# One decoder step on one core: padded queries copied by VectorE, and a causal mask moved out of the matrix products of the state-space mixer

## The chip, the core and the metric

The program runs on one core of one Trainium2 chip. The metric is the device time of one execution in microseconds, the median of three runs, and lower is better. The engines of the core run beside each other, each through its own queue in order: TensorE (PE, with its weight loads PEld), VectorE (DVE), ScalarE (ACT), GpSimd (POOL) and SyncE (SP, which here only issues transfers). An instruction that waits holds up all that stands behind it in its queue.

## What is computed

The reference is one step of a two-layer decoder over 512 prompt tokens and 8 sample tokens, 520 columns in all. Layer 0 mixes tokens by sparse attention with 16 heads, layer 1 by a Mamba-2 scan with 32 heads; each mixer is followed by a squared-ReLU MLP. Of the attention, the change touches the prompt's two masked score products (selected keys and window keys), and of the scan this:

```python
seg = a_cum[:, :, :, None] - a_cum[:, :, None, :]
decay = jnp.exp(jnp.where(causal, seg, NEG))
cb = jnp.einsum('bclgn,bcsgn->bclsg', cc, bc)
y_diag = jnp.einsum('bclsg,bclsgr,bcsgrp->bclgrp', cb, decay, xdt)
...
final, prev = lax.scan(step, init_state.astype(f32), ...)
y_off = jnp.einsum('bclgn,bcgrpn,bclgr->bclgrp', cc, prev, jnp.exp(a_cum))
```

For a sample the scan is one step: state = state * exp(dt a) + (x dt) B, and y = sum over n of state * C.

## The kernel before, in words

All products with weights split each weight tile into a high and a low fp32r part (`split`, lines 407 and after: ACT writes `hi`, DVE writes `lo`, tiles `wh`) and multiply three times (`unit`, L323). One product of 1024 by 128 weights is 48 matmuls that write a tile `a`; two such tiles and six `wh` tiles exist. The instructions of each engine are put in order by a scheduler when the program is built, so that the order of the queues is not the order of the code; a change in one stage reorders others.

**Attention** (`attention`, L1021, one item for each of 8 head pairs `i`, 4 query tiles `t` of 128 and 2 halves `e`, 64 items). `att_qk` (L937) makes the scores of an item: for both key sets one product with the high keys (`sc<-kv,q`), one with the low keys (`sc<-kv,c`), and the mask as a product of the identity with `negqR` (`sc<-c,c`). The low keys of two heads lie in one tile, so the second product takes queries that are zero in the other head's 64 rows: a padded tile `qz[e]`, 128 by 128, into which POOL copies the 64 rows of this item (L945, `c<-q`). There is one such tile for each `e`, so a copy waits for the products of the item two before. POOL also issues the stores of cached keys and values (`out_kwin`, L357) and the loads of the selected pages (`wh<-in_selv`, L395). `att_soft`, `att_scale`, `att_tr` and `att_pv` follow some items later; the sample group's attention and the modulation products are woven in.

**Mixer** (`ssd`, in the order of `SSD_SEQ`: four groups `bc`, each with four pairs of heads). `ssd_bc` (L1465) computes B, C and `cb`, the product of B and C by chunks of 128 tokens. `ssd_pair` (L1507) does one pair `q` of heads, 16 in all:

- Two PSUM tiles `ps[e]`, each the cumulated decay spread over 128 rows by a product with one column of `e2R`, plus the mask as a product of the identity with `negsR`: four matmuls of 512 columns (`s<-c,c`).
- For each head four ACT operations `M<-s,c` (exponential with the negated decay `nac` as bias, 128 columns each), then one DVE product `M<-M,g` with `cb`.
- POOL builds `sp`, and one matmul of 384 columns (`s<-c,sp`) gives the decay of both heads for their own 64 rows, of which ACT takes the exponential `E`.
- Then the transposes of X (`s<-c,x`), the chunk states (`s<-xd,g`), the diagonal part (`s<-M,xd`), the off-diagonal part (`s<-g,st`).
- For each of the 8 samples: ACT scales B (`xb<-bc,x`), DVE updates the state (`ss<-ss,c,xb`, L1463) and multiplies it by C with an accumulated sum (`xb,ys<-ss,bc`), 128 elements each. The sums `ys` enter the sample columns of `y`.

`ssd_gate` multiplies `y` by the gate `z` (`y<-y,z`), squares it and splits it into `yh` for the output products; after the last pair the norm of the mixer (`s<-c,yss`, `s<-c,z`) needs all of `y`. The PSUM pool `s` has four tiles.

Of the kernel before, what the change touches and what calls it, by code (L numbers as in the profile page):

```python
# [11 lines left out]
F32R = mybir.dt.float32r  # L12
# [15 lines left out]
_o = 0  # L30
# [6 lines left out]
def shape_constants():  # L37
    c = np.zeros((128, NCONST), np.float32)

    def put(name, a):  # L40
        o, w = CONST_AT[name]
        c[:a.shape[0], o:o + w] = a

    i = np.arange(128)
    put('ident', np.eye(128, dtype=np.float32))
    put('negq', np.where(i[None, :] <= i[:, None], 0.0, NEG))
    put('tri', (i[:, None] <= i[None, :]).astype(np.float32))
    put('negs', np.where(i[:, None] <= i[None, :], 0.0, NEG))
    t = np.arange(4)[None, :, None] * 128 + i[:, None, None]
    ok = (16 * np.arange(32)[None, None, :] + 31 <= t) & (np.arange(32) < 31)  # L50
    put('cadd', np.where(ok, 0.0, NEG).reshape(128, 128))
    put('cmul', ok.astype(np.float32).reshape(128, 128))
    j, hc = i // 32, i % 32
    gp, r, e = hc // 8, (hc // 2) % 4, hc % 2
    live = hc < 16
    g = 2 * gp + e
    b = np.arange(8)
    put('selb', np.stack([(b[:, None] == 4 * k + j[None, :]) & live[None, :] for k in range(2)], 1)
        .astype(np.float32).reshape(8, 256))
    put('gsel', ((np.arange(16)[None, :] == (g * 4 + r)[:, None]) & live[:, None]).astype(np.float32))  # L60
# [201 lines left out]
class Step:  # L262
# [391 lines left out]
    def setup_late(self):  # L654
        I = self.I
        wg = self.tile('s', [128, 384])
        self.aux(wg, I['w_gate'])
        self.wg = [self.tile('kv', [128, 384], F32R) for _ in range(2)]
        self.copy(self.wg[0], wg)
        self.tt(self.wg[1], wg, self.wg[0], ALU.subtract)  # L660
        t = self.tile('s', [128, 256])
        self.aux(t[:, 0:128], I['const'][:, CONST_AT['negq'][0]:CONST_AT['negq'][0] + 128])
        self.aux(t[:, 128:256], I['const'][:, CONST_AT['negs'][0]:CONST_AT['negs'][0] + 128])
        self.negqR = self.const([128, 128], F32R, self.pn)
        self.vcopy(self.negqR, t[:, 0:128])
        self.negsR = self.const([128, 128], F32R)
        self.vcopy(self.negsR, t[:, 128:256])
        u = self.U('np')
        self.load_consts(u[:, 0:256], 'selb', 'selb', self.aux)
        self.gt = u[:, 256:448].rearrange("p (a b) -> p a b", a=4)  # L670
        self.load_consts(self.U('np'), 'cadd', 'jc', self.aux)
# [265 lines left out]
    def att_qk(self, n):  # L937
        i, t, e = n
        gp = i // 4
        w = (t + 1) * 128  # L940
        q = self.Q[i][e][:, t * 128:(t + 1) * 128]
        r = slice(64 * e, 64 * e + 64)

        qz = self.qz[e]
        self.nc.gpsimd.tensor_copy(qz[r], q[r])  # L945
        one = self.tile('sc', [128, 2, 256]) if w <= 256 else None
        self.S[n] = []
        for k in range(2):
# [73 lines left out]
    def attention(self, fill, rate):  # L1022

        items = [(i, t, e) for i in range(8) for t in range(4) for e in range(2)]
        N = len(items)
        self.S, self.P, self.PT = {}, {}, {}
        self.qz = [self.const([128, 128], F32R, self.pn) for _ in range(2)]
        for z in self.qz:
            self.nc.gpsimd.memset(z.bitcast(F32), 0.0)
        cg = [self.att_cmp(i) for i in range(0, 8, 2)]  # L1030
        for n in range(N + PV + 1):
            if n < N:
                i, t, e = items[n]
                next(cg[n // 16], None)
                self.att_qk(items[n])
            if 0 <= n - TR < N:
                self.att_tr(items[n - TR], 0)
            m = n - PV
            if 0 <= m < N and m % 2 == 1:
                self.att_pv(items[m][0], items[m][1])  # L1040
            if 0 <= n - TR < N:
                self.att_tr(items[n - TR], 1)
            if n < N:
                self.att_soft(items[n])
            if 0 <= n - 1 < N:
                self.att_scale(items[n - 1])
            fill.step(rate)
# [310 lines left out]
    def dt_fin(self, ps):  # L1358
# [47 lines left out]
        self.copy(ac, p[:, 0:128])  # L1406

        m = self.m[0].rearrange("p a b -> p (a b)")
        self.nac, self.cd, self.dtde = (m[:, ck(n)].rearrange("p (c h) -> p c h", c=4) for n in range(3))
        fl = "p c h -> p (c h)"  # L1410
        self.ts(self.nac.rearrange(fl), p[:, 0:128], -1.0)
        self.copy(ae, p[:, 128:256])
        self.act(self.cd.rearrange(fl), p[:, 128:256], AF.Exp)
        self.tt(ae, ae, ac, ALU.subtract)
# [50 lines left out]
    def ssd_bc(self, g, first):  # L1465
# [7 lines left out]
        for c in range(4):  # L1473
            self.mm(p[:, ck(c)], B[:, ck(c)], C[:, ck(c)], True, True)
        cb = self.tile('g', [128, 512])
        self.copy(cb, p)
        p = self.tile('s', [128, 512])
        for c in range(4):
            self.tr(p[:, ck(c)], B[:, ck(c)])
# [24 lines left out]
    def ssd_pair(self, g, t, X, G, w):  # L1504
# [4 lines left out]
        M = []  # L1509
        ps = [self.tile('s', [128, 512]) for _ in range(2)]  # L1510
        for e in range(2):
            self.mm(ps[e], self.e2R[:, 2 * q + e:2 * q + e + 1].to_broadcast([128, 128]), self.ac2, True, False)
        for e in range(2):
            self.mm(ps[e].rearrange("p (c l) -> p c l", c=4), self.identR,
                    self.negsR[:, None, :].to_broadcast([128, 4, 128]), False, True)
        for e in range(2):
            h = 2 * q + e
            p = ps[e]
            m = self.tile('M', [128, 512])
            for c in range(4):  # L1520
                self.act(m[:, ck(c)], p[:, ck(c)], AF.Exp, bias=self.nac[:, c, h:h + 1])
            self.tt(m, m, cb, ALU.mult)
            M.append(m)
        sp = self.tile('sp', [128, 2, 64], F32R)
        self.nc.gpsimd.tensor_copy(sp, self.e2R[:, 2 * q:2 * q + 2, None].to_broadcast([128, 2, 64]))
        p = self.tile('s', [128, 512])
        self.mm(p[:, 128:512], sp.rearrange("p a b -> p (a b)"), self.ac2[:, 128:512], True, True)
        E = self.tile('E', [128, 512])
        self.act(E[:, 128:512], p[:, 128:512], AF.Exp)

        p = self.tile('s', [128, 512])
        for c in range(4):
# [44 lines left out]
        for b in range(8):  # L1577
# [1 line left out]
            x = self.tile('xb', [128, 128])  # L1579
            self.act(x, bc[0][:, b], AF.Copy, scale=x8[:, b:b + 1])  # L1580
            self.pool_stt(v, v, self.sdb[:, q, 1, b:b + 1], x, ALU.mult, ALU.add)
            self.stt(x, v, 1.0, bc[1][:, b], ALU.mult, ALU.mult, accum_out=ys[:, b:b + 1])
        self.store(self.O['ssm_s'][q], w.rearrange("p b n -> p (b n)"))
        self.stt(y[:, 512:T], xs[:, 2 + t], self.dsk[:, q:q + 1], ys, ALU.mult, ALU.add)
        return y
# [295 lines left out]
    def build(self, stop=None):  # L1881
        self.make_plan()
        base = {'n': 1, 'r': 1}
        with self.phase('n', {'kv': 16, 'np': 9, 's': 5, 'pcm': 1, 'ptc': 1, 'ptsc': 1, 'ad': 1, 'sq': 1, 'ssq': 1, 'x7': 's'}) \
                as self.pn, self.phase('np', {'t': 2, 'o': 1, 'f': 1}, PSUM):
            ap = contextlib.ExitStack()
            ap.enter_context(self.products_phase('ap1'))
# [11 lines left out]
        with self.tc.tile_pool(name='e', bufs=1) as self.pe:  # L1899
# [4 lines left out]
                    return  # L1904
                h = self.boundary(('n', 'r'), BOUND_CGS[1], 'f')
            with self.phase('s', {'g': 5, 'cv': 2, 'x': 2, 'th': 2, 'xd': 3, 'st': 2, 'M': 2, 'E': 1, 'y': 1, 'z': 1,
                                  'acc': 8, 'bc': 1, 'ss': 2, 'xb': 3, 'yss': 1, 'yh': 8, 'sp': 1,
                                  'sq': 'M', 'x7': 'M', 'ssq': 'st', 'ad': 'xd', 'dt': 'acc'}) as self.ps, \
                    self.phase('sp', {'s': 4}, PSUM), self.products_phase('ap4'), \
                    self.tc.tile_pool(name='dr', bufs=2, space=bass.MemoryType.DRAM) as self.pd:  # L1910
# [59 lines left out]
```

## Time and profile before

| | us |
|---|---|
| median of 3 runs | 1711.87 (1711.11 to 1712.05) |
| the profiled execution, its own time | 1709.68 |
| its span, first to last instruction | 1708.0 |
| PE busy in the span | 1661.1 (97%) |
| DVE busy | 978.6 (57%) |
| ACT busy | 762.3 (45%) |
| POOL busy | 117.9 (7%) |

The span of the profile is the time between the first and the last instruction; the execution's own time has 1.7 us around it. The attention lies from about 207 to 420 us, the first MLP to 870, the pairs of the mixer from 917 to 1282, the second MLP from 1320 on. Busy times of PE are modelled from pipelined matmuls: two matmuls overlap in the record, and what one costs the queue is read from the distance of two starts.

### The profile page before, as it was taken

The page shows a single profiled execution, that of the slowest core. Times are in us where ns is not written, and L with a number is a line of the kernel's source. Part 1 is how long each engine was busy: PE and PEld are TensorE (multiplying, and loading weights), DVE is VectorE, ACT ScalarE, POOL GpSimd, SP SyncE. Part 2 cuts the span into 40 slices and gives each one's busy share as a digit, 9 for nine tenths or more (in the row PEclk, how much of TensorE's full clock was granted, in tenths as well). Part 3 has the DMA queues.
Part 4 walks back from the last instruction along what each step waited for, and adds up shares of the span by engine and source line. Part 5 has one row for each costly group of instructions (what it writes and reads, how often), then busy time and mean ns, then how long its engine had stood idle before and what let it go on. Part 6 is the DMA issues. An engine that isn't in the chain of part 4 may idle for free.

```text
span 1708.0 us, 34635 instructions
## 1 busy us (share of the span) xinstructions
PE 1661.1 (97%) x13846; PEld 1544.8 (90%) x13846; DVE 978.6 (57%) x2442; ACT 762.3 (45%) x1624; POOL 117.9 (7%) x284
## 2 busy tenths in 40 slices
PE   7999999999999999999999999999999999999997
PEld 6799876667989999999989999999997999999997
DVE  2543377776464343433469977979797543434344
ACT  3534376666443132322446766647564432323231
POOL 2000112310000000000001101101010000000000
PEclk9999999999999999999999999999999999999999
DMA  9723656545433524244433352343425223323221
GB/s 323 270 87 100 216 201 227 167 143 196 139 116 107 175 97 136 87 136 136 136 131 119 105 181 83 128 143 129 144 79 183 70 92 88 98 87 99 87 87 51
DMA packets 72114, 229.87 MB, mean 135 GB/s; under 512 B 8770, under 2 KB 15218, under 8 KB 71186
## 3 DMA queue, kind: packets, MB, share of 16 engines
q1 hardware_dynamic: 62546, 198.45, 35.2%
q0 software_dynamic: 8832, 28.16, 4.5%
q8 instruction: 109, 1.79, 0.4%
q10 hardware_dynamic: 576, 1.05, 0.2%
q14 instruction: 51, 0.42, 0.1%
HBM read 204.02 MB, written 23.61 MB: 133 GB/s over the span
## 4 chain that ended last, share of the span: by engine, by line
PE 76%; DVE 2%; issue 1%; ACT 1%; SPq 1%; POOLq 0%; DMA 0%; POOL 0%; DVEq 0%; ACTq 0%
PE a L323 64%; PE s L323 5%; PE f L323 2%; PE o L323 1%; PE sc L323 1%; PE t L327 1%; PE s L327 1%; DVE c L345 0%; SPq L395 0%; SPq L393 0%; POOLq L393 0%; PE f L327 0%; DVE g L345 0%; DMA w<-in_selk_dram 0%; DVE wh L336 0%
## 5 line engine op out<-in xcount | busy, mean ns | idle before, releaser
L323 PE MATMUL a<-h,wh 128*128 128x256 f32 x5952 | 746.6, 285 | 5.9 <-ACT t L333 1.6
L323 PEld LDWEIGHTS a<-h,wh 128*128 128x128 f32 x5952 | 726.9, 190 | 13.1 <-issue 3.8
L330 ACT ACTIVATE wh<-w 128x1024 fp32r<-128x1024 f32 x212 | 224.6, 1060 | 513.7 <-PE a L323 479.3
L336 DVE TENSOR_TENSOR wh<-w,wh 128x1024 fp32r<-128x1024 f32 x212 | 259.6, 1224 | 269.8 <-ACT wh L330 266.8
L323 PEld LDWEIGHTS a<-hid,wh 128*128 128x128 f32 x3072 | 370.2, 188 | 5.0 <-issue 4.2
L323 PE MATMUL a<-hid,wh 128*128 128x256 f32 (+1 forms) x3072 | 373.6, 283 | 0.0
L336 DVE TENSOR_TENSOR t<-a,c 128x8 f32<-128x8 f32 x72 | 12.0, 166 | 215.8 <-PE a L323 215.8
L323 PE MATMUL a<-yh,wh 128*128 128x256 f32 (+1 forms) x768 | 98.4, 285 | 0.3 <-DVE acc L336 0.3
L323 PEld LDWEIGHTS a<-yh,wh 128*128 128x128 f32 x768 | 93.7, 188 | 1.9 <-ACT wh L330 0.8
L330 ACT ACTIVATE hid<-t 128x520 fp32r<-128x520 f32 x64 | 40.8, 639 | 84.5 <-DVE t L336 84.5
L330 ACT ACTIVATE h<-t 128x128 f32<-128x128 f32 (+3 forms) x128 | 52.8, 441 | 51.7 <-PE t L327 51.1
L333 ACT ACTIVATE h<-sc,m 128x128 f32<-128x128 f32 (+3 forms) x128 | 66.6, 529 | 10.4 <-DVE m L340 7.4
L336 DVE TENSOR_TENSOR hid<-t,hid 128x520 fp32r<-128x520 f32 x64 | 44.7, 699 | 42.3 <-ACT hid L330 42.3
L333 ACT ACTIVATE xb<-bc,x 128x128 f32<-128x128 f32 x128 | 45.4, 413 | 29.2 <-DVE xb L345 21.3
L345 DVE SCALAR_TENSOR_TENSOR c<-a,c,c 128x512 f32<-128x512 f32 (+1 forms) x74 | 53.8, 728 | 1.8 <-PE a L323 1.8
L327 PE MATMUL t<-c,h 128*128 128x128 f32 x320 | 53.7, 281 | 0.9 <-DVE h L340 0.4
L327 PEld LDWEIGHTS t<-c,h 128*128 128x128 f32 x320 | 35.1, 141 | 13.8 <-issue 8.6
L323 PE MATMUL sc<-kv,q 128*128 128x128 f32 (+3 forms) x128 | 47.0, 379 | 0.0
L323 PEld LDWEIGHTS a<-q,wh 128*128 128x128 f32 x384 | 46.2, 188 | 0.8 <-issue 0.8
L323 PE MATMUL a<-q,wh 128*128 128x256 f32 (+1 forms) x384 | 46.5, 283 | 0.0
L323 PE MATMUL sc<-kv,c 128*128 128x128 f32 (+3 forms) x128 | 41.3, 334 | 4.3 <-POOL c L945 4.3
L340 DVE TENSOR_SCALAR h<-h,z 128x128 f32<-128x128 f32 (+3 forms) x128 | 44.4, 384 | 1.3
(367 smaller groups left out, 1903.1 us busy)
## 6 DMA issues: line engine op xcount, KB each, us to landing
w<-in_w_dram SPq DMA_DIRECT2D x128, 512.0 KB, 3.5
w<-in_ada_w_dram SPq DMA_DIRECT2D x80, 512.0 KB, 3.6
w<-in_w_ssd_dram SPq DMA_DIRECT2D x40, 512.0 KB, 3.6
w<-in_w_nsa_dram SPq DMA_DIRECT2D x20, 512.0 KB, 3.7
ss<-in_ssm_dram SPq DMA_DIRECT2D x16, 512.0 KB, 4.5
out_ssm_s_dram<-ss POOLq DMA_DIRECT2D x16, 512.0 KB, 3.1
w<-in_w_sout_dram SPq DMA_DIRECT2D x16, 512.0 KB, 4.1
cm<-in_cmp_dram SPq DMA_DIRECT2D x24, 256.0 KB, 4.2
```

Of the source, the lines that this page charges most:

```text
L323: self.nc.tensor.matmul(out, lhsT, rhs, start=start, stop=stop, skip_group_check=True)
L327: self.nc.tensor.transpose(out, in_, self.C('ident')[0:k, 0:k])
L330: self.nc.scalar.activation(out, in_, AF.Copy, **kw)
L333: self.nc.scalar.activation(out, in_, f, **kw)
L336: self.nc.vector.tensor_tensor(out, a, b, op=op)
L340: self.nc.vector.tensor_scalar(out, a, s1, None, op0=op0)
L345: self.nc.vector.scalar_tensor_tensor(out, a, s, b, op0=op0, op1=op1, **kw)
```

## The change

- Attention: the padded tiles are 128 by 256, hold two query tiles, and DVE copies into them ahead, once for two items (`att_pad`): 32 copies of 64 by 256 in place of POOL's 64 of 64 by 128.
- Mixer, mask: `cb` is multiplied by the 0/1 triangle when it leaves PSUM (a DVE product instead of an ACT copy, 4 in all). The mask product with `negsR` goes. So that the exponential can't overflow above the diagonal, ACT first takes Relu of the negated difference, 4 operations a head, and then the exponential of the negated result in one operation of 512 columns.
- Mixer, `E`: ACT takes it from the two `ps[e]` (64 rows each) and not from a product of its own; `sp`, its copy and its matmul go.
- Mixer, samples: the eight products with C become one DVE operation of 1024 elements into a tile `vc` and one DVE sum. `xb` has 2 buffers instead of 3.
- Room: `negsR` goes, `ptsc` shares the buffer of `ad`.

```diff
     def att_qk(self, n):
...
-        qz = self.qz[e]
-        self.nc.gpsimd.tensor_copy(qz[r], q[r])
+        qz = self.qz[e][:, (t % 2) * 128:(t % 2) * 128 + 128]
...
+    def att_pad(self, i, t, e):
+        r = slice(64 * e, 64 * e + 64)
+        self.vcopy(self.qz[e][r], self.Q[i][e][r, t * 128:t * 128 + 256])
...
     def attention(self, fill, rate):
...
+        for e in range(2):
+            self.att_pad(0, 0, e)
...
                 self.att_qk(items[n])
+                if t % 2 and n + 2 < N:
+                    self.att_pad(*items[n + 2])
...
     def ssd_bc(self, g, first):
...
-        self.copy(cb, p)
+        self.tt(cb.rearrange("p (c l) -> p c l", c=4), p.rearrange("p (c l) -> p c l", c=4),
+                self.C('tri')[:, None, :].to_broadcast([128, 4, 128]), ALU.mult)
...
     def ssd_pair(self, g, t, X, G, w):
...
-            self.mm(ps[e], self.e2R[:, 2 * q + e:2 * q + e + 1].to_broadcast([128, 128]), self.ac2, True, False)
-        for e in range(2):
-            self.mm(ps[e].rearrange("p (c l) -> p c l", c=4), self.identR,
-                    self.negsR[:, None, :].to_broadcast([128, 4, 128]), False, True)
+            self.mm(ps[e], self.e2R[:, 2 * q + e:2 * q + e + 1].to_broadcast([128, 128]), self.ac2, True, True)
...
-                self.act(m[:, ck(c)], p[:, ck(c)], AF.Exp, bias=self.nac[:, c, h:h + 1])
+                self.act(m[:, ck(c)], p[:, ck(c)], AF.Relu, scale=-1.0, bias=self.ac[:, c, h:h + 1])
+
+            self.act(m, m, AF.Exp, scale=-1.0)
             self.tt(m, m, cb, ALU.mult)
...
-        sp = self.tile('sp', [128, 2, 64], F32R)
-        self.nc.gpsimd.tensor_copy(sp, self.e2R[:, 2 * q:2 * q + 2, None].to_broadcast([128, 2, 64]))
-        p = self.tile('s', [128, 512])
-        self.mm(p[:, 128:512], sp.rearrange("p a b -> p (a b)"), self.ac2[:, 128:512], True, True)
         E = self.tile('E', [128, 512])
-        self.act(E[:, 128:512], p[:, 128:512], AF.Exp)
+        for e in range(2):
+            r = slice(64 * e, 64 * e + 64)
+            self.act(E[r, 128:512], ps[e][r, 128:512], AF.Exp)
...
-            self.stt(x, v, 1.0, bc[1][:, b], ALU.mult, ALU.mult, accum_out=ys[:, b:b + 1])
+        vc = self.tile('vc', [128, 8, 128])
+        self.tt(vc, w, bc[1], ALU.mult)
+        self.nc.vector.tensor_reduce(ys, vc, AX.X, ALU.add)
```

The scheduler moves instructions in both stages. Three places matter below.

POOL's queue before, at the start of the attention (`c<-q` the padded copy, `out_kwin` a store of cached keys or values):

```order
L357 DMA out_kwin_dram<-wh_3396 128x1024
L945 COPY c_2383<-q_996 64x128
L357 DMA out_kwin_dram<-wh_3402 128x1024
L945 COPY c_2384<-q_997 64x128
L945 COPY c_2383<-q_996 64x128
```

The copies stand behind stores that wait for a load. DVE's queue now, at the same place (`im` and `pcm` belong to other parts of the attention, `m<-sc` is the row maximum of the scores):

```order
L335 TENSOR_TENSOR pcm_2391<-pcm_2391,mcm_2455 128x512
L335 TENSOR_TENSOR im_2476<-im_2476,c_2444 128x12
L347 COPY c_2380<-q_993 64x256
L335 TENSOR_TENSOR c_2444<-c_2444,c_1507 128x64
L965 TENSOR_REDUCE m_2496<-sc_2482 128x2
```

The copy leaves the queue in which it stood behind stores that wait for loads, and stands in DVE's behind small operations; it now serves the third query tile, since the first two are padded before the attention begins.

ACT's queue in the mixer, at the fifth pair, before (`M` a head's decay matrix, `x` a convolution):

```order
L333 ACTIVATE M_12741<-s_12735,c_99 128x128
L333 ACTIVATE x_12718<-cv_12713,c_7351,c_7349 128x512
L333 ACTIVATE M_12741<-s_12735,c_99 128x128 x3
L333 ACTIVATE M_12747<-s_12736,c_99 128x128 x4
L333 ACTIVATE E_12757<-s_12755 128x384
L330 ACTIVATE xd_12766<-s_12759,c_11223 128x64 x8
```

`E` and `xd` follow the eight `M` at once. ACT's queue now, at the same pair:

```order
L332 ACTIVATE M_12672<-s_12668,c_99 128x128
L332 ACTIVATE x_12651<-cv_12646,c_7316,c_7314 128x512
L332 ACTIVATE M_12672<-s_12668,c_99 128x128 x3
L332 ACTIVATE M_12679<-s_12669,c_99 128x128
L332 ACTIVATE M_12672<-M_12672 128x512
L332 ACTIVATE M_12679<-s_12669,c_99 128x128 x3
L332 ACTIVATE E_12686<-s_12668 64x384
L332 ACTIVATE M_12679<-M_12679 128x512
L332 ACTIVATE E_12686<-s_12669 64x384
L332 ACTIVATE th_12656<-x_12651 128x512
L332 ACTIVATE cvt_12663<-xs_12277 128x8
L329 ACTIVATE xd_12696<-s_12689,c_11188 128x64 x8
```

Three more operations stand between a pair's first `M` and the `xd` that its diagonal product also needs, and PE's queue holds more products with weights between the `s<-c,c` and the first `s<-M,xd` of a pair: 42 where 19 stood at this pair, 57 where 29 stood at the last.

DVE's queue at the last pair of the mixer before (`y<-y,z` is the last product with the gate):

```order
L1463 SCALAR_TENSOR_TENSOR ss_16460<-ss_16460,c_11288,xb_16564 128x128
L345 SCALAR_TENSOR_TENSOR z_16625<-z_16625,a_16576 128x520
L345 SCALAR_TENSOR_TENSOR xb_16564,ys_16535<-ss_16460,bc_15334 128x128
L345 SCALAR_TENSOR_TENSOR y_16529<-xs_15164,c_7358,ys_16535 128x8
L336 TENSOR_TENSOR y_16529<-y_16529,z_16625 128x520
```

One product with C and the gate's first step lie between the last state update and `y`. DVE's queue now, at the same pair:

```order
L1466 SCALAR_TENSOR_TENSOR ss_16305<-ss_16305,c_11253,xb_16399 128x128
L335 TENSOR_TENSOR vc_16402<-ss_16305,bc_15203 128x1024
L335 TENSOR_TENSOR wh_16485<-w_16476,wh_16484 128x1024
L1585 TENSOR_REDUCE ys_16377<-vc_16402 128x8
L344 SCALAR_TENSOR_TENSOR y_16371<-xs_15033,c_7323,ys_16377 128x8
L335 TENSOR_TENSOR y_16371<-y_16371,z_16462 128x520
```

Three operations of 1024 elements, one of them a weight split, stand between the last state update and the last `y<-y,z`, where two small ones of this pair and the gate's stood. In PE's queue 22 products with weights stand between the last `s<-M,xd` and the norm's `s<-c,z`, where 55 stood before.

## Rows read from the trace of the kernel before

**Rows 1.** The page: busy time by engine, and the chain that ended last.

```profile
PE 1661.1 (97%) x13846; PEld 1544.8 (90%) x13846; DVE 978.6 (57%) x2442; ACT 762.3 (45%) x1624; POOL 117.9 (7%) x284
...
PE 76%; DVE 2%; issue 1%; ACT 1%; SPq 1%; POOLq 0%; DMA 0%; POOL 0%; DVEq 0%; ACTq 0%
```

**Rows 2.** Stretches: length, busy PE, PEld, DVE, ACT, POOL (instructions), clock, DMA, GB/s.

```profile
207.00:420.00 213.00, 203.68 (x1872) 143.22 (x1870) 158.00 (x578) 139.17 (x442) 46.94 (x123) 0.99 0.55 192
212.80:216.20 3.40, 3.36 (x15) 3.36 (x15) 0.99 (x5) 0.57 (x3) 1.34 (x4) 0.51 0.78 316
917.00:1000.00 83.00, 81.44 (x673) 77.50 (x671) 77.85 (x236) 59.34 (x163) 10.02 (x24) 1.00 0.42 144
1020.00:1103.00 83.00, 82.80 (x678) 79.17 (x677) 67.05 (x183) 53.17 (x139) 9.05 (x21) 1.00 0.37 122
917.00:1282.00 365.00, 363.06 (x2990) 345.95 (x2989) 313.20 (x918) 230.32 (x602) 40.44 (x87) 1.00 0.37 126
```

**Rows 3.** Waits of PE in the attention: us in total, times, longest.

```profile
PE sc L323 <- POOL c L945: 4.3, 2, 2.9
PE t L327 <- DVE h L340: 0.4, 1, 0.4
```

**Rows 4.** Timeline at both waits for POOL: start, length, engine, what, [idle before].

```profile
211.34 0.53 POOL L357 DMA_DIRECT2D out_kwin_dram<-wh  x1 [4.12 <-DMA wh<-in_winv_dram]
211.92 0.87 POOL L945 CAST c<-q 64x128 fp32r<-64x128 f32 x1
212.53 0.29 DVE L336 TENSOR_TENSOR im<-im,c 128x12 f32<-128x12 f32 x1
212.84 0.58 PE L323 MATMUL sc<-kv,c 128*128 128x256 f32 x1 [2.90 <-POOL c L945]
...
307.97 0.50 PE L323 MATMUL sc<-kv,c 128*128 128x512 f32 x1 [1.43 <-POOL c L945]
```

**Rows 5.** Timeline of PE at one pair.

```profile
1051.11 1.09 PE L323 MATMUL s<-c,c 128*128 128x512 f32 x4
1052.04 0.34 PE L323 MATMUL s<-c,sp 128*128 128x384 f32 x1
1052.22 0.60 PE L327 MATMUL s<-c,x 128*128 128x128 f32 x4
```

**Rows 6.** Timeline of DVE: sample products and a weight split.

```profile
1052.02 0.28 DVE L345 SCALAR_TENSOR_TENSOR xb<-ss,bc 128x128 f32<-128x128 f32 x1
1052.23 0.28 DVE L345 SCALAR_TENSOR_TENSOR xb<-ss,bc 128x128 f32<-128x128 f32 x1
1052.44 1.21 DVE L336 TENSOR_TENSOR wh<-w,wh 128x1024 fp32r<-128x1024 f32 x1
1053.58 0.16 DVE L348 COPY c<-a 128x8 f32<-128x8 f32 x1
```

**Rows 7.** Groups of the page and by shape: count, busy us, mean ns of one.

```profile
L323 PE MATMUL a<-h,wh 128*128 128x256 f32 x5952 | 746.6, 285 | 5.9 <-ACT t L333 1.6
L345 DVE SCALAR_TENSOR_TENSOR xb<-ss,bc 128x128 f32<-128x128 f32 x128 | 33.5, 284 | 0.1
L345 DVE DVE_READ_ACCUMULATOR xb<-ss,bc 128x1 f32 x128 | 10.3, 80 | 0.0
L336 DVE TENSOR_TENSOR wh<-w,wh 128x1024 fp32r<-128x1024 f32 x212 | 259.6, 1224 | 269.8 <-ACT wh L330 266.8 <-DMA w<-in_w_nout_dram 1.5 <-PE s L323 0.8
L340 DVE TENSOR_SCALAR h<-h,z 128x256 f32<-128x256 f32 x32 | 9.9, 346 | 0.2
```

**Rows 8.** Timelines of ACT and PE at the last pair.

```profile
1267.85 0.58 ACT L333 ACTIVATE z<-a 128x520 f32<-128x520 f32 x1
1268.33 2.17 ACT L333 ACTIVATE M<-s,c 128x128 f32<-128x128 f32 x8
...
1282.82 0.64 ACT L333 ACTIVATE z<-y 128x520 f32<-128x520 f32 x1 [2.62 <-DVE y L336]
1285.88 1.28 PE L323 MATMUL s<-c,z 128*128 128x1 f32 x10
```

More of the change, by code (lines that the diff above doesn't have):

```diff
@@ L23 @@
 NEG = -1e30
-CONST_COLS = [('ident', 128), ('tri', 128), ('e2', 32), ('negq', 128), ('negs', 128), ('selb', 256),
+CONST_COLS = [('ident', 128), ('tri', 128), ('e2', 32), ('negq', 128), ('selb', 256),
               ('cadd', 128), ('cmul', 128), ('gsum', 128), ('gsel', 16), ('gmask', 4), ('sel2', 16), ('jc', 6)]
@@ L47, in shape_constants @@
     put('tri', (i[:, None] <= i[None, :]).astype(np.float32))
-    put('negs', np.where(i[:, None] <= i[None, :], 0.0, NEG))
     t = np.arange(4)[None, :, None] * 128 + i[:, None, None]
@@ L660, in setup_late @@
         self.tt(self.wg[1], wg, self.wg[0], ALU.subtract)
-        t = self.tile('s', [128, 256])
+        t = self.tile('s', [128, 128])
         self.aux(t[:, 0:128], I['const'][:, CONST_AT['negq'][0]:CONST_AT['negq'][0] + 128])
-        self.aux(t[:, 128:256], I['const'][:, CONST_AT['negs'][0]:CONST_AT['negs'][0] + 128])
         self.negqR = self.const([128, 128], F32R, self.pn)
         self.vcopy(self.negqR, t[:, 0:128])
-        self.negsR = self.const([128, 128], F32R)
-        self.vcopy(self.negsR, t[:, 128:256])
         u = self.U('np')
@@ L941, in att_qk @@
         q = self.Q[i][e][:, t * 128:(t + 1) * 128]
-        r = slice(64 * e, 64 * e + 64)
-        qz = self.qz[e]
-        self.nc.gpsimd.tensor_copy(qz[r], q[r])
+        qz = self.qz[e][:, (t % 2) * 128:(t % 2) * 128 + 128]
         one = self.tile('sc', [128, 2, 256]) if w <= 256 else None
@@ L1026, in attention @@
         self.S, self.P, self.PT = {}, {}, {}
-        self.qz = [self.const([128, 128], F32R, self.pn) for _ in range(2)]
+        self.qz = [self.const([128, 256], F32R, self.pn) for _ in range(2)]
         for z in self.qz:
             self.nc.gpsimd.memset(z.bitcast(F32), 0.0)
+        for e in range(2):
+            self.att_pad(0, 0, e)
         cg = [self.att_cmp(i) for i in range(0, 8, 2)]
@@ L1408, in dt_fin @@
         m = self.m[0].rearrange("p a b -> p (a b)")
-        self.nac, self.cd, self.dtde = (m[:, ck(n)].rearrange("p (c h) -> p c h", c=4) for n in range(3))
+        self.ac, self.cd, self.dtde = (m[:, ck(n)].rearrange("p (c h) -> p c h", c=4) for n in range(3))
         fl = "p c h -> p (c h)"
-        self.ts(self.nac.rearrange(fl), p[:, 0:128], -1.0)
+        self.vcopy(self.ac.rearrange(fl), p[:, 0:128])
         self.copy(ae, p[:, 128:256])
@@ L1883, in build @@
         base = {'n': 1, 'r': 1}
-        with self.phase('n', {'kv': 16, 'np': 9, 's': 5, 'pcm': 1, 'ptc': 1, 'ptsc': 1, 'ad': 1, 'sq': 1, 'ssq': 1, 'x7': 's'}) \
+        with self.phase('n', {'kv': 16, 'np': 9, 's': 5, 'pcm': 1, 'ptc': 1, 'ptsc': 'ad', 'ad': 1, 'sq': 1, 'ssq': 1, 'x7': 's'}) \
                 as self.pn, self.phase('np', {'t': 2, 'o': 1, 'f': 1}, PSUM):
@@ L1906, in build @@
             with self.phase('s', {'g': 5, 'cv': 2, 'x': 2, 'th': 2, 'xd': 3, 'st': 2, 'M': 2, 'E': 1, 'y': 1, 'z': 1,
-                                  'acc': 8, 'bc': 1, 'ss': 2, 'xb': 3, 'yss': 1, 'yh': 8, 'sp': 1,
+                                  'acc': 8, 'bc': 1, 'ss': 2, 'xb': 2, 'yss': 1, 'yh': 8, 'vc': 1,
                                   'sq': 'M', 'x7': 'M', 'ssq': 'st', 'ad': 'xd', 'dt': 'acc'}) as self.ps, \
```

## The prediction, made before the change ran

> **What bounds the kernel now.** I read the page first, then the busy times by stretch, then the waits and timelines of the two stretches that the change touches. The reader should see in [rows 1] that PE is busy for 97% of the span and carries 76% of the chain that ended last, so work taken out of PE's queue is worth its full length wherever nothing else comes last. Then [rows 2]: in the attention PE is busy 203.68 of 213 us, DVE 158.00, ACT 139.17. Over the mixer's pairs PE is busy 363.06 of 365 us, and DVE, off the chain, is busy 313.20. The first group of pairs (917 to 1000) is the dense one: DVE 77.85 of 83 us, 94%, against 67.05 in the second group. So in the mixer PE sets the pace with DVE close behind, and a change that relieves PE and loads DVE has to be counted on both.
>
> **Attention: POOL leaves the path.** PE waited 4.3 us for POOL's padded copy, two times [rows 3]. The first wait, 2.90 us, is a queue effect: the copy stood behind a store that waited 4.12 us for the load of its data [rows 4]. What comes last in its place? PE would run on through the second query tile, whose padded queries are then long there, and next need the third tile's copy, which now stands behind `im<-im,c`. That ended at 212.82, just before PE resumed at 212.84 [rows 4]. So part of the wait only moves to the third tile: I take 2.0 of the 2.90 us as gained; ends 0 and 2.9.
>
> [...] I take 0.8; ends 0 and 1.7. The second wait, 1.43 us [rows 4], has POOL's page loads ahead of the copy and should go whole: 1.4; it could be late on DVE too, so ends 0 and 1.4.
>
> DVE gets 32 copies of 64 by 256. No row shows one; the nearest is a DVE operation on 128 by 256 at 346 ns, above it, and a 128 by 8 copy at 0.16 us below [rows 6, 7]. I take 0.30 us, nearer to the upper row since the element count is the same: 9.6 us on an engine that has 55 us free here. PE waited 0.4 us for DVE's scaling in this stretch [rows 3], so most is covered; I charge 1.0 us to the path, ends 0 and 4. POOL's 64 copies go; nobody else waited for them. Sum of the attention: -2.0 - 0.8 - 1.4 + 1.0 = **-3.2 us**.
>
> **Mixer: the matmuls that go.** Four mask and decay products start at 1051.11, the next instruction at 1052.04, so 0.93 / 4 = 0.2325 us each; the 384-column product takes 0.18 us to the next start [rows 5]. Removed are 2 and 1 for each of 16 pairs: 32 x 0.2325 + 16 x 0.18 = 7.4 + 2.9 = **10.3 us** of PE's queue. This is the largest term, and it stands if nothing else comes last.
>
> **Mixer: DVE.** By starts, a sample product with C occupies DVE for 0.21 us (1052.02 to 1052.23, 1052.23 to 1052.44), its accumulator read included, and an operation of 128 by 1024 for 1.14 us (1052.44 to 1053.58) [rows 6]. Eight go, 1.68 us a pair; a product and a sum of 1024 come, 2.28 us: +0.60 a pair, +9.6 over 16 pairs. The four `cb` products of 512 columns, half of the 1.14 each, add 2.3. So DVE gains some 12 us of work, against what the shorter code suggests. Of rows that give only durations one would have found the reverse: 8 x (284 + 80 ns) = 2.91 us against 2 x 1224 ns = 2.45 [rows 7]; but those overlap in the record, so I go by starts.
>
> [...]
>
> Where do the 12 us land? In the second and later groups DVE had 16 us of 83 free, which covers the 3.0 us that a group gets (4 x 0.60 + 0.6) and the 2.6 us that PE saves there. In the first group only 5 us were free [rows 2], and 3.0 more work in a time that should shrink by 2.6 does not fit: I charge **+2.5 us**, ends 0 (the free 5 us suffice) and 5.6.
>
> **Mixer: ACT and the pair's chain.** By starts, a 128 by 520 operation takes 0.48 us and eight `M` 2.0 us [rows 8]. A pair gets two exponentials of 512 columns and one more `E`, below 0.48: some 1.3 us longer before `xd` and the diagonal product; 16 x 1.3 = 21 us on ACT, which had 135 us free [rows 2]. The order answers with more products between a pair's decay and its diagonal product (42 instead of 19, 57 instead of 29), each 746.6 / 5952 = 0.125 us [rows 7], so 23 x 0.125 = 2.9 us of cover for 1.3. I charge 0 for the pairs inside.
>
> **The last pair** has no such stock behind it. 33 products fewer (55 to 22) stand between its diagonal product and the norm, 33 x 0.125 = 4.1 us less cover, and DVE's tail there grows by 0.6. The square that the norm reads was finished at 1282.82 + 0.64 = 1283.46, and PE read it at 1285.88 [rows 8]: 2.4 us were to spare. 4.1 + 0.6 - 2.4 = **+2.3 us**, ends 0 and 4.7. The dropped copy of `sp`, the smaller setup and the shared `ptsc` lie beside other work; the cover is PE's own products; without it `ptsc` would cost one wait of about one large DVE operation, 1.14 us.
>
> **Sum.** -3.2 - 10.3 + 2.5 + 2.3 = -8.7 us. Against the profiled execution's 1709.68 us that is 1701.0; the median of the runs lies 2.2 us above that execution, so I forecast 1711.87 - 8.7 = **1703.2 us**.
>
> **Rivals.** [...] *The attention gains nothing*: DVE's copies come as late as POOL's did and put 4 us on the path, and the mixer gains 5.5: -1.5, 1710.4 us. For it, DVE's `im` operation at the first wait; against it, 0.4 us of waits for DVE. *Slower*: PE, in order, stands at each pair's diagonal product because relu, exponential and `E` in ACT's queue make `M` and `xd` late, 1.3 us a pair uncovered: the forecast's -8.7 less the tail's 2.3 and 0.9 of the DVE charge, which the same waits would cover, plus 16 x 1.3 = 20.8, is +8.9, 1720.8 us. It decides from 8.7 / 16 = 0.54 us of new wait a pair. Against it speaks the order's 23 to 28 more products ahead.
>
> **Chances.** Forecast 0.52, nothing given back 0.27, no gain in the attention 0.13, slower 0.08. A run of this kernel tells about 0.2%, 3.4 us, from no change: faster 0.79, same 0.13, slower 0.08. The range takes in the full-gain case and the no-gain case: 1695.5 to 1711; about 0.2 lies outside.
>
> **What would show it.** Right: no wait for POOL in the attention; 48 matmuls fewer in the `s` groups and the pairs' stretch some 5 us shorter; DVE above 95% in the first group; a wait of PE for ACT or DVE of some 2 us just before the norm of the mixer. Wrong: waits of PE at `s<-M,xd` in every pair (slower rival), DVE busy falling in the mixer (first rival), or a wait for DVE's copy at `sc<-kv,c` (second).

## The result, and the profile after

The changed kernel takes **1722.35 us** (median of 11 runs, 1719.13 to 1730.79) against 1711.11 for the kernel before, measured beside it (11 runs, 1703.68 to 1721.44). The ratio is **1.0069, 95% interval 1.0051 to 1.0087**: slower by 0.7%, 11 us, where 8.7 us faster was forecast. The profiled execution took 1724.08 us, its span 1722.4.

The page, busy time and chain, as [rows 1]:

```profile
PE 1661.5 (96%) x13798; PEld 1539.6 (89%) x13798; DVE 997.5 (58%) x2253; ACT 787.6 (46%) x1668; POOL 84.8 (5%) x203
...
PE 86%; DVE 5%; ACT 5%; DMA 1%; issue 1%; SPq 1%; DVEq 0%; ACTq 0%; POOL 0%
```

PE runs 48 matmuls fewer and is as long busy as before. DVE and ACT now hold 5% of the chain each, where they held 2% and 1%. Stretches, as [rows 2] (the same columns), and three more at stalls:

```profile
207.00:420.00 213.00, 204.82 (x1856) 142.12 (x1855) 163.84 (x604) 138.23 (x439) 27.16 (x60) 0.98 0.54 191
917.00:1000.00 83.00, 77.81 (x625) 73.92 (x624) 75.67 (x172) 59.97 (x157) 5.85 (x19) 0.96 0.37 126
1020.00:1103.00 83.00, 80.16 (x646) 76.28 (x645) 66.25 (x139) 52.40 (x124) 6.54 (x16) 0.98 0.35 119
917.00:1290.00 373.00, 362.78 (x2943) 342.11 (x2941) 320.43 (x690) 253.73 (x643) 28.56 (x72) 0.99 0.36 123
339.00:345.80 6.80, 3.55 (x10) 0.57 (x6) 0.81 (x4) 0.18 (x2) 2.15 (x4) 0.71 0.93 305
974.00:980.80 6.80, 2.20 (x10) 2.23 (x11) 6.18 (x16) 3.90 (x10) 0.72 (x2) 0.71 0.24 87
1295.00:1301.70 6.70, 2.95 (x14) 2.95 (x15) 3.91 (x6) 2.80 (x4) 0.00 (x0) 0.70 0.65 239
```

PE stands for some 5 us in the first group of pairs, and the granted clock falls at each of the last three stretches, 0.71, 0.71 and 0.70 in the mean of 7 us. What it waited for most in the mixer's groups, 900 to 1300 (us in total, times, longest), first in the kernel before, then now:

```profile
PE a L323 <- DVE c L348: 1.4, 1, 1.4
PE a L323 <- DVE acc L336: 0.3, 1, 0.3
```

```profile
PE a L322 <- ACT xb L332: 5.0, 1, 5.0
PE s L322 <- ACT z L332: 3.8, 1, 3.8
PE a L322 <- DVE c L347: 2.2, 1, 2.2
PE s L322 <- ACT xd L329: 2.0, 7, 0.4
```

One more wait lies behind the norm, at the statistics of the next stage (1300 to 1345; before, then now):

```profile
PE s L323 <- DVE st L336: 2.0, 1, 2.0
PE s L322 <- DVE st L335: 4.6, 1, 4.6
```

It is 2.0 us in att_only below and 4.4 to 4.7 us in every kernel that has the mask part, whatever else was changed; what made it longer was not tested.

**A measure for the mixer alone.** Profiles with the same attention code differ there by 10 us (last section), so I compare stages. Weight products (48 matmuls `a<-...,wh`, 212 products in all) come in the same number and order in all kernels here. From the start of product 80, in the first MLP, to product 160, in the second, lies the whole mixer: 598.5 us before (797.6 to 1396.1), **611.3 now** (798.9 to 1410.2), +12.8. In parts: products 92 to 104 (the first group) 104.5 to 107.6, 104 to 140 259.1 to 265.4, 140 to 148 (the last pairs, the norm and the statistics behind it) 82.3 to 86.9; the two ends changed by +0.6 and -2.0. In the attention, from product 16 to 20, 248.1 became 249.9. Each kernel has one profile; two kernels with the same mixer code agree in this measure to 1.2 us or less (four such pairs in the experiments), so differences of 1 or 2 us say little.

Where the time went, by starts between products 92 and 148 (445.9 us before, 460.0 now): the removed matmuls took 10.4 us with them; PE's waits of over 0.15 us grew from 6.0 to 21.2; and the same weight products and `s<-M,xd` took 10.2 us more, 358.6 before and 368.8 now, with the granted clock at 0.50 for 27 us in place of 12; all else took 0.9 us less.

### The profile page after: what moved, and what is told of

It reads as the page before. It is cut to its first block, busy times and chain, and to the rows that moved or that the text cites. A ratio compares the mean times of both kernels' runs of the same rounds, so it can differ in the third digit from the quotient of the medians.

```text
span 1722.4 us, 34206 instructions
## 1 busy us (share of the span) xinstructions
PE 1661.5 (96%) x13798; PEld 1539.6 (89%) x13798; DVE 997.5 (58%) x2253; ACT 787.6 (46%) x1668; POOL 84.8 (5%) x203
## 4 chain that ended last, share of the span: by engine, by line
PE 86%; DVE 5%; ACT 5%; DMA 1%; issue 1%; SPq 1%; DVEq 0%; ACTq 0%; POOL 0%
PE a L322 69%; PE s L322 4%; PE f L322 3%; PE sc L322 3%; PE o L322 3%; PE t L326 2%; ACT M L332 1%; DVE wh L335 1%; DMA cm<-in_cmp_dram 1%; PE f L326 1%; PE t L322 1%; ACT h L332 0%; PE s L326 0%; DVE c L344 0%; ACT x L332 0%
## 5 line engine op out<-in xcount | busy, mean ns | idle before, releaser
L322 PE MATMUL a<-yh,wh 128*128 128x256 f32 (+1 forms) x768 | 102.1, 289 | 0.8 <-DVE z L344 0.8
L332 ACT ACTIVATE h<-sc,m 128x128 f32<-128x128 f32 (+3 forms) x128 | 66.5, 528 | 13.6 <-DVE m L339 10.9
L322 PE MATMUL o<-h,kv 128*64 128x128 f32 x640 | 45.4, 279 | 0.0
L1466 DVE SCALAR_TENSOR_TENSOR ss<-ss,c,xb 128x128 f32<-128x128 f32 x128 | 41.2, 346 | 6.7 <-ACT xb L332 6.4
```

The lines of the kernel that those rows point to most:

```text
L322: self.nc.tensor.matmul(out, lhsT, rhs, start=start, stop=stop, skip_group_check=True)
L332: self.nc.scalar.activation(out, in_, f, **kw)
L1466: self.nc.vector.scalar_tensor_tensor(out, a, s, b, op0=op0, op1=op1)
```

## Experiments

The theory that I started from: one of the three parts makes the stalls. "Samples" (merged product with C, two `xb` buffers) or "mask" (a longer chain on ACT); the rival was that the attention does it.

### One part at a time

*att_only* (the kernel before plus the diff's `att_pad`, `att_qk`, `qz` and the shared `ptsc`):

> The kernel before with the attention part alone. The trace of the changed kernel has lost the two waits for POOL (4.3 us), yet from the start of the attention to the first weight product behind it 1.9 us more pass, with four waits for DVE's scaling (2.4 us) and a half-clock stretch twice as long. Theory 'the sample part costs the time' and theory 'the mask part costs it' both expect +1 to +3 us here (about 1713), since neither lies in the attention. The prediction's own step would give -3.2 us (1708). More than +5 us would say that the attention carries a good part of the loss.

Measured 1708.83 us, ratio 1.0001 [0.9977, 1.0024]. Mixer measure 597.3 as before, products 16 to 20 246.4 in place of 248.1. So the attention part gains 1.7 us in one profile and nothing that the runs can tell: neither the loss of 1 to 3 us nor the gain of 3.2 was there.

*mask_only* (before plus the parts `cb`, Relu, `E`):

> The kernel before with the mask, the Relu and E alone; samples and attention as before. Theory 'samples' (product with C merged, two xb buffers): the removed matmuls give -10.4 us, the waits of PE for xd take some 2 back, so about 1703. Theory 'mask' (ACT's longer chain and the new order of the pairs make the stalls): the stalls of 5.0, 3.8 and 4.6 us stay, so 1715 or more.

Measured 1721.29, 1.0048 [1.0027, 1.0069]; mixer 605.9, +7.4. That is the mask theory's side in time: with matmuls gone, the mixer is longer. But of the three stalls that the theory named only that of 4.6 us stayed; those of 5.0 and 3.8 are gone.

*no_att* (the changed kernel, attention undone):

> The changed kernel with the attention part undone. Both theories on the mixer expect the time of the changed kernel less the attention's 1 to 3 us: about 1720, with the stalls of the mixer still there. If it falls under 1715 the attention matters by moving the order of the later stages, or more than its own stretch shows.

Measured 1724.15, 1.0066 [1.0038, 1.0093]; mixer 611.2, the changed kernel's. The attention doesn't reach into the mixer.

*no_samples* (the changed kernel with the old eight products and `xb` 3):

> The changed kernel with the sample part undone (eight products with accumulated sums, three xb buffers). Theory 'samples': the stall in the first group, the wait before the norm and most of the 13 us of new stalls and half-clock time go, so 1704 to 1707. Theory 'mask': they stay, 1717 or more.

Measured 1717.55, 1.0033 [1.0011, 1.0054]; mixer 606.8. The stalls of 5.0 and 3.8 us are gone here too. So **the mask part carries +7.4 to +8.3 of the 12.8 us and the samples +4.5 to +5.3**: neither theory alone.

### Inside the mask part

The 16 products `s<-M,xd` of one pair (the eleventh), PE's timeline, in no_samples and in the kernel before:

```profile
1161.68 0.43 PE L322 MATMUL s<-M,xd 128*64 128x128 f32 x2
1162.05 0.86 PE L322 MATMUL a<-h,wh 128*128 128x256 f32 x5
1162.84 0.43 PE L322 MATMUL s<-M,xd 128*64 128x128 f32 x2
1163.20 0.39 PE L322 MATMUL a<-h,wh 128*128 128x264 f32 x1
1163.52 0.44 PE L322 MATMUL s<-M,xd 128*64 128x128 f32 x4
1163.88 0.38 PE L322 MATMUL a<-h,wh 128*128 128x256 f32 x1
1164.20 0.44 PE L322 MATMUL s<-M,xd 128*64 128x128 f32 x4
1164.57 0.51 PE L322 MATMUL a<-h,wh 128*128 128x264 f32 x2
1165.00 0.44 PE L322 MATMUL s<-M,xd 128*64 128x128 f32 x4
1165.37 0.39 PE L322 MATMUL a<-h,wh 128*128 128x264 f32 x1
```

```profile
1162.18 1.09 PE L323 MATMUL s<-M,xd 128*64 128x128 f32 x16
1163.21 0.49 PE L323 MATMUL s<-g,st 128*128 128x128 f32 x2
```

Before, one block of 1.03 us. Now five blocks, 1161.68 to 1165.37: 3.69 us, of which the 9 weight products between are 9 x 0.125 = 1.1, so the pair's own cost is 2.6, +1.5. A block of two takes as long as one of four (0.43 and 0.44 us): the four start two at a time, the two one after the other (in the changed kernel's trace the two of a pair start 0.007 us apart, those of a block of two 0.16 us). Over the mixer there are 47 such blocks where there were 32. ACT's timeline at the same pair:

```profile
1159.77 0.50 ACT L332 ACTIVATE E<-s 64x384 f32<-64x384 f32 x1
1160.14 0.65 ACT L332 ACTIVATE M<-M 128x512 f32<-128x512 f32 x1
1160.81 0.49 ACT L332 ACTIVATE E<-s 64x384 f32<-64x384 f32 x1
1161.32 0.31 ACT L329 ACTIVATE xd<-s,c 128x64 f32<-128x64 f32 x1
1161.53 0.62 ACT L332 ACTIVATE th<-x 128x512 f32<-128x512 f32 x1
1162.05 0.20 ACT L332 ACTIVATE cvt<-xs 128x8 f32<-128x8 f32 x1
1162.15 1.53 ACT L329 ACTIVATE xd<-s,c 128x64 f32<-128x64 f32 x7
```

The `xd` scalings, in step with which PE's blocks come, stand behind the second pass `M<-M` and both `E`, and `E` isn't needed before the off-diagonal part. New theory "order and xd": ACT's queue in front of `xd` costs the time. Rival "PSUM": `E` now reads the two decay tiles and keeps them from the pool of four. Four kernels, all with the attention part and the old samples, to be held against 606.8:

*no_relu* (it leaves out the Relu and the second pass, and takes a quarter of the exponent; `nac` is made with -0.25):

```diff
-                self.act(..., AF.Relu, scale=-1.0, bias=self.ac[...])
-            self.act(m, m, AF.Exp, scale=-1.0)
+                self.act(..., AF.Exp, scale=0.25, bias=self.nac[...])
```

> Attention and mask part as changed, samples as before, but each head has again four exponentials straight from PSUM (scale 0.25, so that nothing overflows; the decay values are left wrong) and no Relu and no second pass. Measure: the time from weight product 80 (first MLP) to weight product 160 (second MLP), 48 matmuls with a weight tile each; it is 598.5 us before, 611.3 in the changed kernel, 606.8 without the sample part. Theory 'order and xd' (the longer chain on ACT makes xd late, and the scheduler breaks the diagonal products into more blocks between weight products, each with a switch, while PE waits at them): about 590 (598.5 - 10.4 + 2). Theory 'PSUM' (E now reads the two decay tiles and keeps them from the four-tile pool longer): no change, 605 to 608.

*relu_sp* (`E` from its own matmul and `sp`, as in the kernel before):

> Attention and mask part as changed, samples as before, but E is taken from its own matmul of 384 columns through sp again; Relu and second pass stay. Same measure (606.8 us with E from the decay tiles). Theory 'PSUM': the decay tiles come free earlier, the stalls go, about 595. Theory 'order and xd': ACT's chain is only one operation shorter, the diagonal products stand in as many blocks, and 16 x 0.18 = 2.9 us of matmuls come back: 606 to 611.

*xd_first* (the block of the transposes and `xd` moved ahead of `ps`):

> Attention and mask part as changed, samples as before, and the same instructions, but the transposes of X and both xd are written ahead of the decay in the pair, so that ACT does the eight xd scalings before Relu and exponentials where it can. Same measure (606.8 us). Theory 'order and xd': the waits for xd go and the diagonal products stand in fewer blocks, 593 to 600, below the 598.5 of the kernel before if the stalls in the first group shrink too. Theory 'PSUM': the decay tiles are held as long, 605 to 609.

*e_late*:

```diff
-        E = self.tile('E', [128, 512])
-        for e in range(2):
-            ...
         p = self.tile('s', [128, 512])
         for c in range(4):
             self.tr(p[:, ck(c)], X[:, ck(c)])
...
         xde, xdt = xd
+        E = self.tile('E', [128, 512])
+        for e in range(2):
+            ...
```

> Attention and mask part as changed, samples as before, and the same instructions, but E is written behind the transposes and xd, so the decay tiles stay in PSUM still longer while ACT reaches xd two operations earlier. Same measure (606.8 us). Theory 'order and xd': 597 to 603. Theory 'PSUM': longer than 606.8, 608 to 612.

| kernel | median, us | ratio to before [95%] | mixer, us | blocks |
|---|---|---|---|---|
| no_samples | 1717.55 | 1.0033 [1.0011, 1.0054] | 606.8 | 47 |
| no_relu | 1708.36 | 0.9978 [0.9948, 1.0008] | 600.0 | 35 |
| relu_sp | 1714.07 | 1.0015 [0.9989, 1.0042] | 599.7 | 53 |
| xd_first | 1712.00 | 0.9996 [0.9973, 1.0018] | 602.5 | 35 |
| **e_late** | **1706.62** | **0.9964 [0.9940, 0.9989]** | **596.6** | 25 |

e_late holds the decay tiles longest and is the fastest: "PSUM" falls as the cause of the loss. With the same instructions in another written order the mixer is 10.2 us shorter; the same pair in e_late, PE and then ACT:

```profile
1156.29 1.09 PE L322 MATMUL s<-M,xd 128*64 128x128 f32 x16
```

```profile
1155.44 0.80 ACT L329 ACTIVATE xd<-s,c 128x64 f32<-128x64 f32 x3
1156.03 1.01 ACT L332 ACTIVATE E<-s 64x384 f32<-64x384 f32 x2
```

"Order and xd" holds in direction. Between products 104 and 140, at a granted clock of 1.00, e_late is 8.0 us shorter than no_samples; waits of over 0.15 us are 1.1 of that, and 7.5 are the starts of the same matmuls (weight products 218.4 to 214.1 us, `s<-M,xd` 15.5 to 12.3). So the price of broken blocks is there, and hardly as waits. But `xd` does not come sooner: from a pair's first `M` to the end of its last `xd` ACT takes 8.5 us in no_samples and 8.1 in e_late (median of 16 pairs). What changed is when PE turns to the block: 0.1 us after the first `xd` and `M` are there in no_samples, so that it goes on in step with ACT, 0.5 us in the kernel before, 2.1 us in e_late. The move of `E` worked through the order that the scheduler gave to PE, and why it gave that order no run shows.

In size the theory was too simple: no_relu and xd_first missed their numbers (600.0 for 590, 602.5 for at most 600), and relu_sp, with the most blocks and 2.8 us of matmuls more, came to 599.7 where 606 to 611 was expected. It pays for its blocks all the same (weight products and `s<-M,xd` 234.7 us between products 104 and 140, 233.9 in no_samples, 226.4 in e_late); it is shorter by 3.3 us of waits there, and most of its 7 us, 4.8, lies behind product 140, where its granted clock was at 0.50 for 10.2 us and no_samples' for 17.1 and another 3.4. Why the clock fell for less time I did not settle.

And of the 10.4 us of matmuls that went, e_late gains only 1.9 in the mixer: its PE waits 13.6 us between products 92 and 148, where it waited 6.0 before. In the first group, where DVE was busy for 94% before, nothing is gained at all (products 92 to 104 took 104.5 us before, 104.9 in no_samples, 104.8 in e_late).

*mask_e_late* (the kernel before plus mask part, `E` late; no attention part):

> The kernel before with the mask part alone and E late; attention and samples as before. Same measure (605.9 us with E in its place, 598.5 before). Theory 'order of E': 594 to 598, and a run at or a little below the kernel before's. Rival 'it needs the attention part too' (another order from the start): 603 or more.

Measured 1708.34, 0.9987 [0.9963, 1.0011]; mixer 595.9, against 605.9 in mask_only: moving `E` in the code is enough by itself, 10.0 us, and the two runs' intervals lie apart.

### Inside the sample part

*after_e_late* (the changed kernel with `E` late):

> The changed kernel, all three parts, with one block of code moved: E is written behind the transposes and xd. Measure: the time from weight product 80 to weight product 160 (598.5 us before, 611.3 in the changed kernel, 606.8 without the sample part, 596.6 without the sample part and with E late). Theory 'order' (the loss of the mask part is the order that the scheduler gives; that of the sample part is its own stalls, 4.4 us): 600 to 602, and the run 4 to 6 us slower than that of E late with the old samples (1706.6). Rival 'the two parts' losses have one cause': 596 to 598. Rival 'E late helps only with the old samples': 607 or more.

Measured 1712.96, 1.0008 [0.9984, 1.0032]; mixer 603.3, just above the 600 to 602 of "order": 8.0 below the changed kernel and 6.7 above e_late. The sample part's cost is its own.

The largest stall, 973.6 to 978.6, is put down to `xb` of ACT, which does not read the product tile `a` that PE waits for. DVE's timeline there shows another candidate, which ends 0.15 us before PE goes on: the copy `c<-a` of a convolution's 8 sample columns, which does read it; it stood behind eight operations:

```profile
974.62 0.70 DVE L335 TENSOR_TENSOR yss<-yss,z 128x520 f32<-128x520 f32 x1 [1.48 <-ACT z L332]
975.24 0.76 DVE L344 SCALAR_TENSOR_TENSOR yh<-y,c,yh 128x520 fp32r<-128x520 f32 x1
975.91 0.55 DVE L335 TENSOR_TENSOR E<-E,s 128x384 f32<-128x384 f32 x1
976.38 0.74 DVE L344 SCALAR_TENSOR_TENSOR y<-x,c,s 128x512 f32<-128x512 f32 x1
...
978.29 0.16 DVE L347 COPY c<-a 128x8 f32<-128x8 f32 x1
```

*after_scact* (`self.vcopy(self.SC[...])` in `conv` becomes `self.copy`, so ACT does it) and *e_late_scact* (the same in e_late):

> The changed kernel with one copy moved from DVE to ACT: the 8 sample columns of a convolution out of the product tile, for which PE waited 5.0 us in the first group (the copy stood in DVE's queue behind yss, yh, E, y and three state updates). Theory 'DVE's queue holds the product tile': the stalls at 978.6 and 1092 us (5.0 and 2.2 us) and the half clock after them go, some 8 us: same measure 603 to 605. Rival 'the two xb buffers make the stall' (PE waits for the convolution's other readers behind the scalings of B on ACT): 609 to 612.

> Attention and mask part with E late, samples as before, and the convolution's copy of 8 sample columns on ACT. Same measure (596.6 us without it). In that run PE still waited 2.6 and 0.8 us for this copy, with half clock after the first: 592 to 595 if DVE's queue holds the product tile, 596 to 598 if another reader does.

after_scact: the two waits of 5.0 and 2.2 us are gone, products 92 to 104 take 101.9 in place of 107.6. So DVE's queue held the tile, and the releaser named by the profile was the wrong one. But the mixer is 607.3, not 603 to 605 (1720.05, 1.0052 [1.0026, 1.0078]), because other waits come:

```profile
PE s L322 <- ACT z L332: 5.6, 1, 5.6
PE a L322 <- DVE wh L335: 2.9, 2, 1.6
```

In the first group, just behind product 104, PE now waits for DVE's weight splits themselves, 2.9 us in two waits; DVE, busy for 75.67 of the 83 us from 917 to 1000 in the changed kernel, is the bound there. e_late_scact says the same, 597.0 (1706.90, 0.9974 [0.9957, 0.9992]), in the range that was to speak for another reader: the wait for the copy went, one of 2.6 us for `wh` came, and nothing was won.

*e_late_half3* (products of four samples each, `vc` half as large, `xb` 3), *e_late_xb2* (the old products, `xb` 2) and *vc_pool* (after_e_late with `vc` by `nc.gpsimd.tensor_tensor`):

> Attention and mask part with E late, and the samples' product with C as two operations of 512 elements and two sums, with three xb buffers. Same measure (596.6 us with the old eight products). If the loss of the sample part comes from one long chain at the end of a pair and from two xb buffers: 595 to 598. If merged products cost by their own length on DVE (0.60 us a pair more): 599 to 603.

> Attention and mask part with E late, the old eight products with C, but two xb buffers in place of three. Measure: the time from weight product 80 to weight product 160 (596.6 us with three buffers, 603.3 with the merged product and two). Theory 'buffers' (ACT's scalings of B and DVE's state updates wait for each other, and that holds what stands behind them): 600 to 603. Theory 'length on DVE' (two operations of 1024 elements at the places where PE waits for DVE): 596 to 599.

> The changed kernel with E late and the merged product with C on POOL, the sum still on DVE, two xb buffers. Same measure (603.3 us with the product on DVE). DVE has 1.14 us a pair less than that, and 0.54 less than with the old eight products. Theory 'length on DVE': the stall of 5.2 us in the first group shrinks to that of the old products (2.6) or less, 597 to 600. Theory 'chain at the end' (the sums come late because the product waits for all eight states): the product takes longer on POOL, the norm waits longer than 3.4 us, 603 or more.

Mixer 601.0, 599.0 and 606.7 (runs 1711.01, 1.0001 [0.9980, 1.0021]; 1709.25, 0.9990 [0.9960, 1.0020]; 1719.57, 1.0076 [1.0047, 1.0106]). The loss of the third buffer costs 2.4 us, at the upper end of the "length" theory's range; merged products cost 4.3 on top of that and 4.4, in halves, with three buffers. On POOL the product takes 2.56 us. The large stall falls to 1.6 us, as "length" says, and the wait before the norm grows from 3.1 to 5.2, as "chain" says; the time, 606.7, is in the range of "chain". DVE's `xd` is late too, four waits of 6.2 us, so vc_pool does not divide the two cleanly. The last pair of the changed kernel shows the chain, DVE then ACT:

```profile
1293.54 1.23 DVE L335 TENSOR_TENSOR vc<-ss,bc 128x1024 f32<-128x1024 f32 x1
1294.69 1.22 DVE L335 TENSOR_TENSOR wh<-w,wh 128x1024 fp32r<-128x1024 f32 x1
1295.82 1.21 DVE L1585 TENSOR_REDUCE ys<-vc 128x8 f32<-128x1024 f32 x1
1297.07 0.23 DVE L344 SCALAR_TENSOR_TENSOR y<-xs,c,ys 128x8 f32<-128x8 f32 x1
1297.33 0.70 DVE L335 TENSOR_TENSOR y<-y,z 128x520 f32<-128x520 f32 x1
```

```profile
1298.06 0.64 ACT L332 ACTIVATE z<-y 128x520 f32<-128x520 f32 x1 [3.79 <-DVE y L335]
```

From the end of the last state to the start of the last `y` 3.8 us pass, and PE had 22 products to fill it, 22 x 0.125 = 2.8 us.

## Why the prediction was wrong

- **Matmuls that go, -10.3 us: right.** By starts, the decay products fall from 15.35 to 7.72 us and 2.82 us of `s<-c,sp` go: 10.45.
- **ACT and the pair's chain, 0 us: the step that failed.** It read the added products between a pair's decay and its diagonal product as 2.9 us of cover for 1.3 us of ACT. ACT's own share was right: busy 253.7 us over the pairs for 230.3, +23 where 21 were counted. The cover was not. The mask part alone was +7.4 where -10.4 were counted: 17.8 us given back. 10.0 of them went with the written place of `E` alone (mask_only to mask_e_late), most of it as broken blocks, and 7.4 us are waits that mask_e_late still has between products 92 and 148 and the kernel before has not (13.4 for 6.0), 2.7 of them at the next stage's statistics. The mistake was to count PE's stock of products and not where the diagonal product stood in it, and to look for a price only in waits: PE waited for `xd` 2.0 us in all, seven times, but it met the `xd` as they came, in broken blocks, 2.6 us for the 16 products of a pair in five blocks where one block took 1.03. The rows of ACT's order ahead of the prediction show both `E` in front of `xd`; they went into the 1.3 us, and the 1.3 us were charged at nothing.
- **DVE, 12 us more work, +2.5 with ends 0 and 5.6: right in place, too small.** A `vc` and a `ys` take 1.14 and 1.13 us by starts, 1.14 assumed. Products 92 to 104 grew by 3.1 us although matmuls went there, 2.7 of it by the samples (104.9 in no_samples). But the sign "DVE above 95%" did not come: it was busy 75.67 of 83 us, 91%, where it had been 94%. The price came as one short copy behind eight operations, 5.0 us; with the copy on ACT (after_scact) 2.9 us of waits for DVE's own weight splits stood in its place. Merging did not relieve DVE: the old operation did product and sum in one pass over 128 elements, 0.21 us, and the new pair passes over all 1024 twice, 0.60 us more a pair of heads; the sample part costs 4.5 us, and 4.3 to 4.4 where products alone are merged.
- **The last pair, +2.3: mis-sized.** The norm waited 3.8 us, and the clock was 0.70 around it; products 140 to 148 took 4.6 us more, and 2.6 us of waits in them are the statistics behind the norm, which the prediction did not count.
- **Attention, -3.2: right in mechanism, too large.** Both waits for POOL are gone, the copies take 0.284 us each (0.30 assumed), and four waits for `h` of DVE, 2.4 us, stand where 1.0 was charged. No run shows the 0.8 us taken for the clock behind the first wait; what the traces show is a granted clock of 0.51 for 3.4 us there in the kernel before, and over 211.5 to 238 one of 1.00 in the changed kernel and in att_only and of 0.55 in xd_first. att_only gains 1.7 in its profile, all of this included, and its runs show no gain. In the changed kernel's own profile it is +1.8, since PE's wait for `w<-in_selk_dram`, 3.2 us (2.9 before), was now followed by a granted clock of 0.50 (342.8 to 346.4) where 1.00 followed it before (344.4 to 348.0).
- **The rivals.** "Nothing is given back", given 0.27, did not come: the mixer is 12.8 us longer, and DVE was busy for 320.43 us over the pairs where it had been for 313.20. "Slower", given 0.08, came out at 1720.8 us, near the measured 1722.35, and its place was right: the pair's diagonal product, behind ACT's longer queue. Its price was not: 1.3 us of wait a pair was assumed, and it came as blocks, stalls and clock, with 4.5 us from the samples; that the numbers lie so near is luck. "The attention gains nothing" was right for the attention in the runs of att_only, and wrong for the mixer.

Faster than both kernels: **e_late**, 0.9964 [0.9940, 0.9989]; attention and mask parts, `E` late, samples left as they were.

## What to carry to other kernels

Write whatever is wanted late (`E` here) behind what the bound engine needs soon: with a scheduler, the same instructions in another written order were worth 10 us. Then look at the order that came of it. When a wait doesn't show, look at how the order has broken up the blocks of the busy engine: 16 products cost 1.0 us in one block and 2.6 in five. And see whether the next engine has room in the very stretch where work leaves the bound engine: of 10.4 us of matmuls that went, e_late gained 1.9 in the mixer and nothing in the first group, where DVE had been busy for 94%. Small pieces on a full engine can be better than a long one that others stand behind: with `E` late and three `xb` buffers the mixer took 596.6 us with eight products and 601.0 with two.

## What was not expected of the hardware

The same attention, the same wait ahead, another clock. att_only and xd_first have the same code for it, and in both PE's last longer stop before was 0.68 us for `h` of DVE; the stretch 211.5 to 238 then ran so (columns as in [rows 2]), first att_only, then xd_first:

```profile
211.50:238.00 26.50, 25.38 (x237) 18.37 (x237) 21.95 (x92) 19.48 (x62) 3.07 (x6) 1.00 0.46 170
```

```profile
211.50:238.00 26.50, 26.06 (x143) 16.98 (x143) 13.59 (x56) 13.08 (x40) 1.06 (x2) 0.55 0.13 53
```

237 matmuls against 143 in the same time, at a granted clock of 1.00 and of 0.55; products 16 to 20 took 246.4 and 256.4 us. Of the 16 profiles beside that of the kernel before, mask_only, no_att, xd_first, after_scact, e_late_half3 and mask_e_late show it, with and without POOL's waits. By that difference, an estimate, such a stretch can account for some 10 us of the spread of single executions (1703 to 1724 us for the kernel before): of the 116 that were measured beside the experiments, those over 1718 us have a mean clock of 0.980 to 0.985 and those under 1710 us 0.988 to 0.993. What sets it off stays open.

With `vc` on POOL, some of DVE's own operations got longer: `M<-M,g` had a mean of 797 ns in vc_pool and 685 in after_e_late, in the same 32 operations:

```profile
L335 DVE TENSOR_TENSOR M<-M,g 128x512 f32<-128x512 f32 x32 | 25.5, 797 | 0.2 <-ACT M L332 0.2
```

```profile
L335 DVE TENSOR_TENSOR M<-M,g 128x512 f32<-128x512 f32 x32 | 21.9, 685 | 0.2 <-ACT M L332 0.2
```

The mean hides what happened. Thirty of the 32 took 0.68 us as before; two took 2.5 us, and both began while POOL's product ran and ended 0.55 us after it:

```profile
1064.38 2.40 POOL L1584 TENSOR_TENSOR vc<-ss,bc 128x1024 f32<-128x1024 f32 x1 [1.96 <-DVE ss L1466]
1064.82 2.52 DVE L335 TENSOR_TENSOR M<-M,g 128x512 f32<-128x512 f32 x1
```

Three weight splits of DVE that began 0.4 to 0.8 us into such a product went the same way, 2.7 to 3.0 us in place of 1.22.
